# Attention by pairs of heads: 256-column sums over the keys and one bias matmul per span

## The chip, the cores and the metric

The kernel runs on one core of one Trainium2 chip. The metric is the device time of one execution in microseconds (us). A core has TensorE (PE, whose weight loads are shown as PEld), VectorE (DVE), ScalarE (ACT), GpSimd (POOL) and SyncE (SP, which here issues most DMAs). Each engine takes its instructions strictly in the order in which the program lists them.

## The reference, cut to what matters

One decoder block on 1024 tokens of width 1024: an RWKV-7 time mix and a sparse attention run in parallel, are merged, and a product-key expert mixer (PEER) follows. The change touches the attention alone:

```python
kv_sel = c_kv[sel]                     # 256 chosen keys of one shared latent, 8 heads of queries
logits = einsum('bqhd,bqkd->bqhk', qb, kv_sel) * 128 ** -0.5 + rel_bias[t5_bucket(tpos - sel)]
p = softmax(where(valid, logits, -inf))
out = einsum('bqhk,bqkd->bqhd', p, kv_sel)
```

The kernel computes it densely: all causal keys, with a mask that removes those not chosen. All 8 heads share the same keys and values (the latent), so only the queries and the bias differ from head to head.

## The kernel before, in words

The sequence is worked in two halves H of 512 tokens, each of four tiles of 128 queries. In each half, the projections of the input come first (`zphase1`, `zphase2`: weights from HBM, split into a high and a low float32r part by ACT and POOL, and three matmuls on 512 columns for each 128 of depth, lines 424 to 426). Then two kinds of work are listed side by side: `rwkv`, the recurrent mix, whose steps depend on each other (8 chains per half, started 4 steps apart by `staggered`), and `attn`, one generator for each tile and head. Sixteen further projections of `zphase2` (the merge gates) are listed between the heads. After that, `merge_b` projects the attention's output (again lines 424 to 426, eight projections of 24 matmuls), and `merge` needs the output of the last RWKV tile (`rwkv_out`, lines 783 to 812). In the second half, gathers of expert rows (POOL issues, DVE products, line 1395) are tied to steps of `rwkv`. The last half of the time is the dense part of the expert mixer (lines 1290 to 1294).

The program lists the work in this order, but a list scheduler with a clock of its own then sets the order on each engine, so a change in one place moves instructions elsewhere. On PE the order that results is fixed: a matmul that waits holds up all behind it.

`attn(i, h, ap, mask)` does one head of tile i. Its first half: logits of 128 queries against (i+1)*128 keys in spans of at most 512 (line 952, queries `q` stationary), the relative bias of the last two tiles of keys added by one matmul per tile (line 955, `back` stationary), mask and row minimum on DVE (line 958), the exponential and the scaling on ACT (lines 961, 963). Its second half, listed two heads later: each 128x128 block of the probabilities `p` is transposed on PE into a PSUM bank `tp` (line 970), four blocks are copied by ACT to `pT` (line 972; all such copies stand under line 233 in the profile, that of the helper), and one matmul per tile of keys adds up the output, with the values `ckv` stationary and 128 columns moving (line 976). The output is copied to `y1` (named y in the profile) and stored (line 980). PSUM has two banks `tp`, shared by logits and transposes, two banks `acc`, shared by projections and this output, and four banks `rw` for `rwkv`.

```python
heads = [attn(i, h, ap, masks[i]) for i in tiles for h in range(8)]
for n in range(34):
    for g in heads[n:n + 1] + heads[max(0, n - 2):max(0, n - 1)]:
        next(g, None)
```

The functions that the change touches, with the line numbers of the profile:

## Time and profile before

| what | us |
|---|---|
| median of 3 runs | 3731.83 |
| lowest and highest run | 3722.95, 3736.19 |
| the profiled execution, its own time | 3729.43 |
| its span (first to last instruction) | 3727.7 |
| mean granted TensorE clock | 0.972 of full speed |

How to read a profile: an engine's busy time is the time in which it has an instruction in work; matmuls overlap, so PE's busy time counts overlapped ones once. A window row gives, for a stretch of the span, the busy time of each engine with the number of its instructions, the granted clock and the share of the DMA engines. A wait row says which instruction waited, for whom, and how long in total. A timeline row gives the start, the time, the engine, the line, the operation with output and inputs, and the number of instructions merged into it. Every float32 matmul of the code stands as two records in the trace, with two weight loads; a float32r matmul (the projections) stands as one.

### The profile page before, as it was taken

How to read it: one execution, taken by the hardware profiler on the slowest of the kernel's cores; microseconds unless marked ns; L12 is line 12 of the kernel's file. 1: busy time of each engine (PE TensorE's matmuls, PEld its weight loads, DVE VectorE, ACT ScalarE, POOL GpSimd, SP SyncE). 2: the span in 40 equal slices, each digit the busy share in tenths (PEclk: the TensorE clock that was granted, in tenths of full speed). 3: DMA queues.
4: the chain of work that ended last, by engine and by line, in shares of the span. 5: the costliest groups of instructions: out<-in, count | busy, mean ns of one | idle time of the engine just before them, and what ended most of it. 6: DMA issues, size and time to landing. Idle time of an engine off the chain costs nothing.

```text
span 3727.7 us, 64789 instructions
## 1 busy us (share of the span) xinstructions
PE 3499.9 (94%) x24045; PEld 3135.1 (84%) x24045; DVE 2587.5 (69%) x5433; ACT 1694.3 (45%) x3230; POOL 1987.4 (53%) x1572
## 2 busy tenths in 40 slices
PE   8999999889999989879999999999999999999997
PEld 7677777666677767669999999999999999999987
DVE  7856653847467764899989985467667776677654
ACT  3649953244344443447676688422222322222223
POOL 5442222354455554336656542467677676777655
PEclk9999999989999999989999999999999999999999
DMA  7453323864667666478888874889989999898873
GB/s 232 151 159 104 107 87 124 291 194 163 215 206 224 213 213 207 135 230 319 318 327 316 316 284 151 300 320 324 339 317 331 332 330 338 320 332 325 306 263 120
DMA packets 436880, 920.95 MB, mean 247 GB/s; under 512 B 36452, under 2 KB 195508, under 8 KB 433876
## 3 DMA queue, kind: packets, MB, share of 16 engines
q1 hardware_dynamic: 311956, 498.38, 39.8%
q0 software_dynamic: 124608, 418.43, 31.5%
q8 instruction: 189, 3.10, 0.3%
q14 instruction: 127, 1.04, 0.1%
HBM read 791.59 MB, written 125.08 MB: 246 GB/s over the span
## 4 chain that ended last, share of the span: by engine, by line
PE 51%; DVE 15%; DMA 12%; ACT 7%; issue 6%; POOL 6%; SPq 0%; POOLq 0%; ACTq 0%; DVEq 0%
PE pair L1294 8%; PE pair L1292 8%; PE pair L1290 8%; PE acc L424 4%; PE acc L425 4%; PE acc L426 4%; DMA g<-in_u_dram,gidx 4%; DMA g<-in_v_dram,gidx 3%; ACT gt L233 3%; POOL g L1391 2%; DMA raw<-in_ut_dram 2%; POOL wlo L1277 2%; DVE g L1395 2%; PE tp L1264 2%; PE acc L976 1%
## 5 line engine op out<-in xcount | busy, mean ns | idle before, releaser
L1277 POOL TENSOR_TENSOR wlo<-raw,whi 128x1024 fp32r<-128x1024 f32 x264 | 648.7, 2459 | 378.2 <-ACT whi L233 354.5
L414 POOL TENSOR_TENSOR wlo<-wraw,whi 128x512 fp32r<-128x512 f32 x280 | 371.1, 1328 | 550.7 <-ACT whi L233 497.2
L233 ACT ACTIVATE whi<-raw 128x1024 fp32r<-128x1024 f32 x264 | 278.9, 1057 | 649.4 <-PE pair L1292 382.9
L1391 POOL DMA_INDIRECT g<-in_u_dram,gidx x361 | 376.6, 1043 | 293.7 <-DVE g L1395 187.6
L1399 DVE SCALAR_TENSOR_TENSOR pg<-g,dots,pg 128x1024 f32<-128x1024 f32 x317 | 407.0, 1284 | 146.0 <-DMA g<-in_v_dram,gidx 143.0
L1290 PE MATMUL pair<-A,whi 128*128 128x320 f32 (+2 forms) x2048 | 480.5, 311 | 25.4 <-DVE A L1322 19.4
L1290 PE MATMUL pair<-h2T,whi 128*128 128x320 f32 x2048 | 475.6, 312 | 15.0 <-ACT whi L233 15.0
L1292 PE MATMUL pair<-A,whi 128*128 128x320 f32 (+2 forms) x2048 | 479.9, 311 | 3.8 <-DVE A L1322 3.6
L1294 PE MATMUL pair<-A,wlo 128*128 128x320 f32 (+2 forms) x2048 | 478.7, 310 | 0.8 <-POOL wlo L1277 0.8
L1292 PE MATMUL pair<-h2T,whi 128*128 128x320 f32 x2048 | 474.7, 311 | 0.0
L1294 PE MATMUL pair<-h2T,wlo 128*128 128x320 f32 x2048 | 473.1, 311 | 1.6 <-POOL wlo L1277 1.6
L1391 POOL DMA_INDIRECT g<-in_v_dram,gidx x320 | 311.7, 974 | 187.4 <-DVE pg L1399 90.7
L424 PE MATMUL acc<-big,whi 128*128 128x512 f32 x864 | 356.6, 414 | 23.1 <-DVE zs L532 6.5
L1290 PEld LDWEIGHTS pair<-A,whi 128*128 128x128 f32 x2048 | 347.4, 189 | 28.0 <-issue 19.9
L1290 PEld LDWEIGHTS pair<-h2T,whi 128*128 128x128 f32 x2048 | 343.9, 188 | 16.9 <-ACT whi L233 15.4
L426 PE MATMUL acc<-big,wlo 128*128 128x512 f32 x864 | 351.8, 408 | 1.7 <-POOL wlo L414 1.7
L425 PE MATMUL acc<-big,whi 128*128 128x512 f32 x864 | 349.9, 405 | 2.4 <-DVE big L450 2.3
L1292 PEld LDWEIGHTS pair<-A,whi 128*128 128x128 f32 x2048 | 347.4, 189 | 5.1 <-DVE A L1322 5.1
L1395 DVE SCALAR_TENSOR_TENSOR g<-g,pg 128x1024 f32<-128x1024 f32 x233 | 281.3, 1216 | 101.3 <-DMA g<-in_u_dram,gidx 100.2
L1294 PEld LDWEIGHTS pair<-A,wlo 128*128 128x128 f32 x2048 | 347.5, 189 | 1.0 <-POOL wlo L1277 1.0
L1294 PEld LDWEIGHTS pair<-h2T,wlo 128*128 128x128 f32 x2048 | 342.9, 188 | 3.4 <-POOL wlo L1277 2.4
L1292 PEld LDWEIGHTS pair<-h2T,whi 128*128 128x128 f32 x2048 | 344.1, 188 | 0.6
(482 smaller groups left out, 6673.1 us busy)
## 6 DMA issues: line engine op xcount, KB each, us to landing
raw<-in_vt_dram SPq DMA_DIRECT2D x136, 512.0 KB, 4.2
raw<-in_ut_dram SPq DMA_DIRECT2D x128, 512.0 KB, 5.5
gtD<-st SPq DMA_DIRECT2D x20, 2048.0 KB, 9.8
gt<-gtD SPq DMA_DIRECT2D x32, 1280.0 KB, 14.5
wraw<-in_wz_dram SPq DMA_DIRECT2D x152, 256.0 KB, 3.2
dotD<-ds SPq DMA_DIRECT2D x69, 320.0 KB, 5.7
al<-dotD SPq DMA_DIRECT2D x69, 320.0 KB, 6.5
mw<-in_wada_dram SPq DMA_DIRECT2D x32, 512.0 KB, 5.4
```

Of the source, the lines that this page charges most:

```text
L233: copy = lambda o, i, **k: A.activation(o, i, AF.Copy, **k)
L414: G.tensor_tensor(lo, raw, hi.bitcast(F32), op=OP.subtract)
L424: mm(pt, lhsT=wh[:, ks], rhs=ah[:, k, :], start=k == 0, stop=False)
L425: mm(pt, lhsT=wh[:, ks], rhs=al[:, k, :], start=False, stop=False)
L426: ins = mm(pt, lhsT=wl[:, ks], rhs=ah[:, k, :], start=False, stop=k == nk - 1)
L1277: G.tensor_tensor(lo, raw, hi.bitcast(F32), op=OP.subtract)
L1290: mm(pts[n], lhsT=wh, rhs=ah[:, h], start=k == 0, stop=False)
L1292: mm(pts[n], lhsT=wh, rhs=al[:, h], start=False, stop=False)
L1294: latest[:] = [mm(pts[n], lhsT=wl, rhs=ah[:, h], start=False, stop=last)]
L1391: G.indirect_dma_start(out=u, out_offset=None, in_=a["u" if n < 2 else "v"], in_offset=bass.IndirectOffsetOnAxis(ap=idx[:, k:k + 1], axis=0))
L1395: V.scalar_tensor_tensor(u, u, 1.0, h2, op0=OP.mult, op1=OP.mult, accum_out=dots[:, k:k + 1])
L1399: V.scalar_tensor_tensor(acc, u, dots[:, k:k + 1], acc, op0=OP.mult, op1=OP.add)
```

## The change

`attn` now takes two heads, 2*h2_ and 2*h2_+1. It does the first half of one head, pauses, does that of the other, pauses, and then does the second half for both. Two tiles of keys of both heads are transposed into one `tp` bank (four blocks, the two heads of a tile of keys side by side) and copied together, and one matmul with 256 moving columns replaces two with 128. The matmuls of the sums now follow each copy, where before they followed all the copies of a head, and the `acc` bank is taken before the first transpose. The bias of both tiles of keys is one matmul on 256 columns where they lie in the same span of 512 (tiles 1, 2, 3, 5, 6, 7); at tile 4 they lie in two spans and stay apart. The output of both heads is one copy and one store; `y1` has one buffer of 256 columns for two of 128. In the list of work, the second half of a pair stands after the first half of the following pair's first head.

```diff
-    def attn(i, h, ap, mask):
+    def attn(i, h2_, ap, mask):
...
+        pts = []
+        for h in (2 * h2_, 2 * h2_ + 1):
...
-            bt = [k for k in (i - 1, i) if k >= 0 and c0 <= k * 128 < c0 + wd]
-            mm(pl[:, :wd], lhsT=q, rhs=ckvT[:, c0:c0 + wd], start=True, stop=not bt)
-            for k in bt:
-                o = 0 if k == i - 1 else 128
-                mm(pl[:, k * 128 - c0:(k + 1) * 128 - c0], lhsT=back, rhs=bias[:, o:o + 128], start=False,
-                   stop=k == bt[-1])
+                b0, b1 = max(c0, (i - 1) * 128), min(c0 + wd, n)
+                mm(pl[:, :wd], lhsT=q, rhs=ckvT[:, c0:c0 + wd], start=True, stop=b0 >= b1)
+                if b0 < b1:
+                    o = b0 - (i - 1) * 128
+                    mm(pl[:, b0 - c0:b1 - c0], lhsT=back, rhs=bias[:, o:o + b1 - b0], start=False, stop=True)
...
+            pts.append(pt)
+            yield
+        py = pacc()
-        for k0 in range(0, i + 1, 4):
-            kn = min(4, i + 1 - k0)
+        for k0 in range(0, i + 1, 2):
+            kn = min(2, i + 1 - k0)
             tp = ptp()
             for k in range(kn):
-                nc.tensor.transpose(tp[:, k * 128:(k + 1) * 128], pt[:, (k0 + k) * 128:(k0 + k + 1) * 128], ident)
+                for e in range(2):
+                    nc.tensor.transpose(tp[:, (2 * k + e) * 128:(2 * k + e + 1) * 128],
+                                        pts[e][:, (k0 + k) * 128:(k0 + k + 1) * 128], ident)
             pT = ap.tile([128, 512], F32, name="pT", bufs=2)
-            copy(pT[:, :kn * 128], tp[:, :kn * 128])
-            pTs.append(pT)
-        py = pacc()
-        for k in range(i + 1):
-            mm(py[:, 0:128], lhsT=ckv[:, k, :], rhs=pTs[k // 4][:, k % 4 * 128:k % 4 * 128 + 128], start=k == 0,
-               stop=k == i)
-        yb = ap.tile([128, 128], F32, name="y1", bufs=2)
+            copy(pT[:, :kn * 256], tp[:, :kn * 256])
+            for k in range(kn):
+                mm(py[:, 0:256], lhsT=ckv[:, k0 + k, :], rhs=pT[:, k * 256:k * 256 + 256], start=k0 + k == 0,
+                   stop=k0 + k == i)
+        yb = ap.tile([128, 2, 128], F32, name="y1", bufs=1)
...
-                heads = [attn(i, h, ap, masks[i]) for i in tiles for h in range(8)]
+                heads = [attn(i, h, ap, masks[i]) for i in tiles for h in range(4)]
                 for n in range(34):
-                    for g in heads[n:n + 1] + heads[max(0, n - 2):max(0, n - 1)]:
-                        next(g, None)
                     if n < 32:
+                        next(heads[n // 2])
                         zphase2(H, act, range(22 + n * (16 - TAIL) // 32, 22 + (n + 1) * (16 - TAIL) // 32))
+                    if n % 2 == 0 and n > 0:
+                        next(heads[n // 2 - 1], None)
```

The order moves in two places of which the prediction speaks. The first is PE's order at tile 7 in the second half. In the rows of the order, `tp` with `ident` and `p` is a transpose, `tp` with `ckvT` a logit matmul, `tp` with `bias` a bias matmul, `acc` with `pT` a sum over the keys, and `rw` belongs to `rwkv`. Before, for one head and the start of a second:

```order
L955 MATMUL tp<-bias,back 128x128 x2
L694 MATMUL rw<-in 64x64 x8
L719 MATMUL rw<-C,bk 128x64 x8
L699 MATMUL rw<-w,in 64x64 x8
L970 MATMUL tp<-ident,p 128x128 x8
L976 MATMUL acc<-pT,ckv 128x128 x4
L952 MATMUL tp<-ckvT,q 128x512
```

In the changed kernel, at the same steps of `rwkv`:

```order
L955 MATMUL tp<-ckvT,q 128x512 x2
L958 MATMUL tp<-bias,back 128x256
L699 MATMUL rw<-w,in 64x64 x8
L975 MATMUL tp<-ident,p 128x128 x8
L980 MATMUL acc<-pT,ckv 128x256 x2
L975 MATMUL tp<-ident,p 128x128
L694 MATMUL rw<-in 64x64 x8
```

The bias matmuls are one, the sums follow after each copy by twos, and the next transposes follow them without logits in between.

The second place is PE's order at the end of the last chain of `rwkv` in the second half: lines 738, 744, 750, 755 and 756 are its last state step, lines 792, 798, 806 and 807 the normalisation and gate of its output, and `acc` with `big` is a projection of `merge_b`. Before:

```order
L738 MATMUL rw<-sv,pr 64x64 x3
L425 MATMUL acc<-big,whi 128x512
...
L744 MATMUL rw<-rh,w 64x64 x4
L424 MATMUL acc<-big,whi 128x512 x2
...
L750 MATMUL rw<-sv,ed 64x64 x4
...
L792 MATMUL rw<-yall,C 128x128 x2
L426 MATMUL acc<-big,wlo 128x512
...
L798 MATMUL rw<-ss,ind_97 8x128 x4
L426 MATMUL acc<-big,wlo 128x512
...
L806 MATMUL rw<-pr,gnx 128x128
```

In the changed kernel, where `acc` with `Q` is the first projection that needs this chain's output:

```order
L738 MATMUL rw<-sv,pr 64x64 x3
L744 MATMUL rw<-rh,w 64x64 x4
L750 MATMUL rw<-sv,ed 64x64 x4
...
L792 MATMUL rw<-yall,C 128x128 x2
L798 MATMUL rw<-ss,ind_97 8x128 x4
L806 MATMUL rw<-pr,gnx 128x128
L807 MATMUL rw<-gl,g_99 128x128
...
L424 MATMUL acc<-Q,whi 128x512 x2
```

The projections that stood between the steps of this chain stand ahead of it. In the first half the order moves in the same way.

## Rows read from the trace of the kernel before

**Rows 1.** The page, part 1: busy time, share of the span, instructions of each engine.

```profile
PE 3499.9 (94%) x24045; PEld 3135.1 (84%) x24045; DVE 2587.5 (69%) x5433; ACT 1694.3 (45%) x3230; POOL 1987.4 (53%) x1572
```

**Rows 2.** Windows: stretch, its length, busy PE, PEld, DVE, ACT, POOL, clock, DMA share.

```profile
300.00:585.00 285.00, 280.83 (x2761) 223.01 (x2761) 161.68 (x470) 209.97 (x526) 76.62 (x82) 0.98 0.35 103
585.00:656.40 71.40, 64.74 (x481) 46.80 (x479) 25.47 (x50) 21.25 (x46) 17.33 (x15) 0.92 0.39 123
656.40:680.00 23.60, 18.60 (x67) 15.04 (x68) 19.59 (x30) 5.25 (x9) 6.00 (x4) 0.79 0.91 311
950.00:1435.00 485.00, 444.64 (x3836) 346.51 (x3834) 311.92 (x701) 218.21 (x473) 246.90 (x211) 0.96 0.68 212
1435.00:1485.00 50.00, 49.20 (x234) 37.18 (x233) 17.05 (x26) 15.99 (x29) 19.14 (x15) 0.97 0.64 211
```

**Rows 3.** Waits of PE from 950 to 1450 us: total, times, longest.

```profile
PE tp L970 <- DVE asm L958: 15.0, 7, 4.0
PE acc L976 <- ACT pT L233: 4.7, 8, 1.1
PE tp L970 <- ACT pT L233: 4.1, 7, 0.7
```

**Rows 4.** Timeline of PE from 343.6 us: projections, logits, bias and transposes in a row.

```profile
343.64 0.40 PE L424 MATMUL acc<-big,whi 128*128 128x512 f32 x1
343.87 0.40 PE L425 MATMUL acc<-big,whi 128*128 128x512 f32 x1
...
344.35 0.59 PE L952 MATMUL tp<-ckvT,q 128*128 128x256 f32 x2
344.78 0.61 PE L955 MATMUL tp<-bias,back 128*128 128x128 f32 x4
345.23 0.38 PE L970 MATMUL tp<-ident,p 128*128 128x128 f32 x2
```

**Rows 5.** Timeline of PE, end of the last RWKV chain in the second half.

```profile
1436.14 0.45 PE L738 MATMUL rw<-sv,pr 128*64 128x64 f32 x6
...
1454.14 1.04 PE L798 MATMUL rw<-ss,ind 128*8 128x128 f32 x8
...
1464.26 0.49 PE L807 MATMUL rw<-gl,g 128*128 128x128 f32 x2
```

**Rows 6.** Timeline of ACT, DVE and POOL: what that chain does between its matmuls.

```profile
1436.62 0.28 ACT L233 ACTIVATE rh<-rw 128x128 f32<-128x128 f32 x1 [2.17 <-PE rw L738]
...
1444.74 0.28 ACT L233 ACTIVATE yall<-rw 128x128 f32<-128x128 f32 x1 [1.98 <-PE rw L756]
...
1450.04 0.58 ACT L793 ACTIVATE ss<-rw 128x512 f32<-128x512 f32 x1
...
1455.53 0.36 ACT L800 ACTIVATE pr<-rw,eps_gn 8x128 f32<-8x128 f32 x1
...
1455.92 0.94 DVE L801 RECIPROCAL pr<-pr 8x128 f32<-8x128 f32 x1 [3.79 <-ACT pr L800]
...
1464.37 0.69 DVE L808 TENSOR_TENSOR yall<-yall,rw 128x512 f32<-128x512 f32 x1 [5.94 <-PE rw L806]
...
1465.13 1.28 POOL L809 TENSOR_TENSOR yall<-yall,ss 128x512 f32<-128x512 f32 x1 [2.81 <-DVE yall L808]
...
1468.72 0.68 DVE L810 TENSOR_TENSOR yall<-yall,rw 128x512 f32<-128x512 f32 x1
...
1469.44 0.63 ACT L233 ACTIVATE Q<-yall 128x512 fp32r<-128x512 f32 x1
...
1470.55 0.68 DVE L450 TENSOR_TENSOR Q<-yall,Q 128x512 fp32r<-128x512 f32 x1
```

**Rows 7.** The page, part 5: the product of a gathered expert row on DVE.

```profile
L1395 DVE SCALAR_TENSOR_TENSOR g<-g,pg 128x1024 f32<-128x1024 f32 x233 | 281.3, 1216 | 101.3 <-DMA g<-in_u_dram,gidx 100.2
```

**Rows 8.** Timeline of PE just after the first half's RWKV: two projection matmuls.

```profile
660.00 0.63 PE L425 MATMUL acc<-Q,whi 128*128 128x512 f32 x1
660.42 0.63 PE L426 MATMUL acc<-Q,wlo 128*128 128x512 f32 x1
```

More of the change, by code (lines that the diff above doesn't have):

```diff
@@ new lines, in attn @@
+        pts = []
+        for h in (2 * h2_, 2 * h2_ + 1):
+            bias = ap.tile([128, 256], F32, name="bias", bufs=2)
+            nc.sync.dma_start(bias, bass.AP(tensor=biasV.tensor, offset=biasV.offset + h * 384, ap=[[1, 128], [1, 256]]))
+            q = ap.tile([128, 128], F32, name="q", bufs=2)
+            nc.sync.dma_start(q, qD[H][h, :, tt * 128:tt * 128 + 128])
+            sm = ap.tile([128, 4], F32, name="asm", bufs=4)
+            pt = ap.tile([128, 512 * (H + 1)], F32, name="p", bufs=3)
+            first = 3.0e38
+            for c0 in range(0, n, 512):
+                wd = min(512, n - c0)
+                pl = ptp()
+                b0, b1 = max(c0, (i - 1) * 128), min(c0 + wd, n)
[3 more added lines that the diff above has]
+                    mm(pl[:, b0 - c0:b1 - c0], lhsT=back, rhs=bias[:, o:o + b1 - b0], start=False, stop=True)
+                j = c0 // 512
+                V.tensor_tensor_reduce(out=pt[:, c0:c0 + wd], in0=pl[:, :wd], in1=mask[:, c0:c0 + wd], op0=OP.add,
+                                       op1=OP.min, scale=1.0, scalar=first, accum_out=sm[:, j:j + 1])
+                first = sm[:, j:j + 1]
+            A.activation(pt[:, :n], pt[:, :n], AF.Exp, scale=-1.0, bias=first, accum_out=sm[:, 2:3])
+            V.reciprocal(sm[:, 3:4], sm[:, 2:3])
+            copy(pt[:, :n], pt[:, :n], scale=sm[:, 3:4])
+            pts.append(pt)
+            yield
@@ L973, in attn @@
-            pTs.append(pT)
-        py = pacc()
-        for k in range(i + 1):
-            mm(py[:, 0:128], lhsT=ckv[:, k, :], rhs=pTs[k // 4][:, k % 4 * 128:k % 4 * 128 + 128], start=k == 0,
-               stop=k == i)
-        yb = ap.tile([128, 128], F32, name="y1", bufs=2)
-        copy(yb, py[:, 0:128])
-        nc.sync.dma_start(ybD[H][h, :, tt * 128:tt * 128 + 128], yb)
+            copy(pT[:, :kn * 256], tp[:, :kn * 256])
+            for k in range(kn):
+                mm(py[:, 0:256], lhsT=ckv[:, k0 + k, :], rhs=pT[:, k * 256:k * 256 + 256], start=k0 + k == 0,
+                   stop=k0 + k == i)
@@ L983, in load_split @@
+        yb = ap.tile([128, 2, 128], F32, name="y1", bufs=1)
+        copy(yb.rearrange("p a b -> p (a b)"), py[:, 0:256])
+        nc.sync.dma_start(ybD[H][2 * h2_:2 * h2_ + 2, :, tt * 128:tt * 128 + 128].rearrange("h p t -> p h t"), yb)
     def load_split(dst, src, n):
```

19 lines of the change are left out of this document (removed).

## The prediction

> **What bounds the kernel now.** I first read the busy times of the whole page [rows 1]: PE is busy for 94% of the span, so the first question is what the change does to PE's own work, and the second what it does to the little time in which PE waits. The window rows [rows 2] then show the two stretches in which attention runs. In the first half (300 to 585 us) PE is busy for 280.83 of 285 us: there nothing is gained by a shorter wait, only by less work. In the second half (950 to 1435 us) it is busy for 444.64 of 485, so 40 us of idle time lie there, and the waits [rows 3] tell how much belongs to attention: 15.0 us in which transposes (line 970) wait for DVE to free a `tp` bank, 4.1 us in which they wait for ACT's copies, and 4.7 us in which sums (line 976) wait for a copy, 23.8 us in all. Last, the timeline gives what a matmul costs [rows 4], and the order of the changed kernel shows what becomes a neighbour of what.
>
> **PE's own work.** Starts tell the cost, since matmuls overlap. One logit matmul on 256 columns stands as two records, from 344.35 to 344.78 us: 0.43, or 0.215 us a record. Two bias matmuls on 128 columns are four records, from 344.78 to 345.23: 0.45, or 0.112 us each [rows 4]. So two 128-column records cost 0.225 us and the 256-column one that replaces them 0.215: 0.010 us saved. Columns, not instructions, are what is paid for. The sums are 36 tiles of keys times 8 heads, 288 matmuls or 576 records, and become 288: 288 times 0.010 = 2.9 us. The bias is joined for 6 tiles and 8 heads, 48 times, 96 pairs of records: 1.0 us. Together 3.9 us of the span, of which I count 3 (between nothing, if the hundredth is rounding, and 4). Logits and transposes stay as they are.
>
> On this point the Trainium skill speaks for more. Its page "TensorE: Matmul & The Clock Gate" (section "Back-to-back issue gap") gives for a stream of weight loads and matmuls about 81 ns at 128 columns and 131 ns at 512, so that a matmul pays a fixed share beside its columns. By a straight line between the two, an estimate, a 256-column matmul would take 98 ns where two of 128 take 162, and 384 pairs would give 25 us instead of 4. The trace differs: 0.215 against 0.225 us.
>
> **Work taken off other engines.** ACT copies 16 fewer `pT` tiles and 32 fewer outputs, and SP issues 32 fewer stores. I cost this at nothing: ACT is busy for 209.97 of 285 us and PE for 280.83 in the first half [rows 2], so what PE does not wait for is hidden beside it. The cover would fail only if PE waited for these copies, and that is in the waits above. One buffer of `y1` makes a pair's output wait for the store before it, one pair earlier, some 17 us in the first half (285 us over 16 pairs) and 30 in the second (485 over 16): nothing. The `acc` bank is held from a pair's first sum to its last, with one bank left for projections; a projection that ends inside must be copied out before the next begins. The order puts at most one projection's worth of 24 matmuls between a pair's first and last sums, so I take nothing here too; one wait of 0.58 us, the time of an ACT pass over 512 columns [rows 6], for each of 32 pairs, 18 us, is the upper end.
>
> **The waits in attention.** A group of transposes that follows logits waits for DVE to read them out of the bank, and the DVE reading may stand behind a product of a gathered row, 1216 ns each [rows 7]. Before, each head's transposes came after another head's logits. Now, as the first place in the order shows, only a pair's first group does; the rest follows the pair's own sums. I take half of the 15.0 us away, 7.5. The new waits, two sums behind their own copy, have the next four transposes, 0.45 us, ahead of them, as the old ones had; I leave these 4.7 and 4.1 us as they are. The bounds are all 23.8 us gone, or as much again if a pair's chained copies stall PE each time.
>
> **The end of each RWKV part.** This is what is late next. The second place in the order shows that, in the changed kernel, attention and projections move ahead of RWKV, and nothing is left to stand between the last steps of the last chain. Before, 80 projection matmuls stand there (counted in the order), at 0.23 us each [rows 4] 18.4 of the 28.6 us from 1436.14 to 1464.75 [rows 5], and PE is busy for 49.20 of 50 us [rows 2]. They are not lost: they run earlier. But what ACT, DVE and POOL do between the chain's matmuls now becomes idle time of PE: 0.28 and 0.28 (copies), 0.58 (square), 0.36 (root), 0.94 (reciprocal), then after the last matmul 0.69, 1.28, 0.68, 0.63 and 0.68 us until the first merge matmul can start. That is 6.4 us [rows 6]; with the hand-overs and the copies of `sv` between lines 744 and 750, for which I allow 1.6, I take 8. The upper end has two gathered products ahead of it on DVE, 2.4 us more [rows 7], and a clock that falls: after the first half's chain, which is already bare before, the granted clock is 0.79 [rows 2], and matmuls start 0.42 us apart [rows 8] instead of 0.23, so one projection of 24 costs 4.6 us more. The upper end is then 15 us.
>
> In the first half the same end has little cover even before: PE is idle for 6.7 of the 71.4 us from 585 to 656.4 [rows 2]. Now 111 projection matmuls (counted in the order), which stood in the steps before it, are gone from there too, and only the tie-breaking of the indexer remains as cover. The last step and the normalisation cost the same 8 us bare, against the 6.7 now, and the step before them about the same two copies and updates, 1 to 2 us: I take 3 more, between nothing and 10.
>
> **The sum.** Less 3 for PE's work, less 7.5 for attention's waits, plus 8 and plus 3 for the two ends: plus 0.5. The profiled execution took 3729.43 us, so the sum gives 3730; it lies 2.4 us below the median of the runs, 3731.83. What is measured is a median, so I forecast 3732: no change. A measurement of this kernel can tell about 0.3%, 11.2 us, from no change, so "same" means 3720.6 to 3743.0 us. The forecast's own range is 3722 to 3742.
>
> **Rivals.** *The ends outweigh the rest (slower).* The mechanism is the bare end of the RWKV chain, in both halves. It costs 15 us in the second half, by its upper end, and 10 in the first; if attention's waits do not shrink, because a pair's four copies in a row stall as often as the logits did, only 3 us are given back. Then 3731.8 + 22 = 3754. It decides from the point at which the two ends together cost some 14 us more than what attention gives back. For it: the order shows no cover at all, and the clock fell in the first half's end. Against it: the chain could only be late if PE had been the one that delayed it, and projections done early are not done later.
>
> *Attention's waits vanish (faster).* With the copies shared and the transposes in larger groups, all but a few of the 23.8 us go, and the chain of the second half, which shares PE with them, ends earlier by as much, which pays for its bare end. Then 3731.8 - 3 - 19 = 3710. For it: the idle 40 us stand just there. Against it: the largest part is DVE's queue, which the change does not shorten.
>
> *Each load is paid for (faster).* If a record of 128 columns hid a fixed cost as large as half of its 0.112 us, 384 of them would give 21.5 us: 3710. This is the rule that I named above, as a mechanism here. The 256-column logits, with one load for 0.215 us, speak against it.
>
> *It moves, and no more.* The order also shifts by a few places after attention, where DVE and POOL serve gathers and expert tables. That could cost or give 10 us or so by itself, with either sign.
>
> **How the numbers follow.** No change, as summed: 0.44. The ends outweigh: 0.30, at about 3754. The waits vanish: 0.18, at about 3710. Loads: 0.02. Later moves decide: 0.06, half to each side. So faster 0.23, same 0.44, slower 0.33. The range takes in the forecast's own case and reaches most of the way to both others: 3711 to 3757.
>
> **What would show it.** In the profile of the changed kernel: sums on 256 columns start 0.215 us a record apart, and PE's busy time is lower by some 3 us, not 20. Transposes wait for DVE for about half of 15 us. Around the last steps of each half's RWKV, PE stands idle between the lines of the last state step and the first merge matmul, for about 8 us in the second half and about 10 in the first. I am wrong if PE's idle time in attention's second stretch falls by more than 15 us, if the bare ends take more than 25 together, or if the difference lies in the dense part.

## The result, and the profile after

| | before | after |
|---|---|---|
| median of 6 runs each, same chip | 3737.62 us | 3786.32 us |
| lowest to highest | 3722.95 to 3741.05 | 3766.11 to 3796.09 |
| span of the profiled execution | 3727.7 | 3788.8 |
| mean granted clock | 0.972 | 0.956 |

The changed kernel is slower: its time is 1.0136 times that of before, 95% interval 1.0115 to 1.0157. The forecast was no change, 3732 us with a range up to 3757; the time lies above the range. The medians differ by 48.7 us, the two profiled executions by 61.1.

The page of the changed kernel, part 1, in the columns of [rows 1]:

```profile
PE 3532.4 (93%) x23661; PEld 3139.7 (83%) x23661; DVE 2584.6 (68%) x5433; ACT 1689.2 (45%) x3181; POOL 1988.6 (52%) x1572
```

384 matmul records fewer, and yet PE is busy for 32.5 us more. More time for fewer instructions goes with the lower granted clock, 0.956 for 0.972. Windows of the changed kernel show where, in the columns of [rows 2]:

```profile
300.00:585.00 285.00, 278.01 (x2510) 215.38 (x2509) 158.44 (x454) 205.81 (x494) 81.38 (x84) 0.99 0.38 110
605.00:662.50 57.50, 48.60 (x390) 35.41 (x388) 21.22 (x46) 16.33 (x38) 6.68 (x6) 0.67 0.27 85
960.90:1510.56 549.66, 501.91 (x3799) 374.22 (x3798) 314.60 (x715) 228.02 (x473) 269.93 (x223) 0.93 0.64 203
1488.00:1510.60 22.60, 15.14 (x80) 10.17 (x78) 9.07 (x18) 7.26 (x14) 6.03 (x5) 0.65 0.48 152
1510.60:1609.40 98.80, 83.30 (x346) 64.72 (x347) 81.13 (x329) 34.69 (x60) 30.61 (x23) 0.89 0.42 132
```

The third row is the second half's attention stage whole, the fourth its end, the fifth the merge behind it. The same three for before (the stage, the merge, the end):

```profile
956.60:1486.00 529.40, 489.58 (x4060) 382.29 (x4059) 322.53 (x720) 232.48 (x500) 262.34 (x222) 0.96 0.68 212
1486.00:1576.30 90.30, 78.47 (x343) 60.30 (x342) 79.17 (x326) 33.88 (x59) 31.53 (x24) 0.96 0.46 145
1435.00:1485.70 50.70, 49.90 (x237) 37.74 (x236) 17.05 (x26) 15.99 (x29) 19.14 (x15) 0.97 0.63 209
```

I cut the span at marks that both kernels have, and compared stage by stage. A stage called "attention" here begins with RWKV (at its first matmul, line 645, in the first half; at the last matmul ahead of it, line 595, in the second) and ends at the first merge projection (`acc` with `Q`). Its length is 529.4 us before and 549.7 after in the second half (+20.3), 417.0 and 426.2 in the first (+9.2). The second half's merge grows by 8.5 (90.3 to 98.8), the layer norm behind it by 3.5; what lies between the first half's stage and the second's is 4.3 us shorter. All that lies behind the layer norm, the expert mixer, is 24.5 us longer in these two executions; the code there is the same, and this part returns below. Of the 20.3 us in the second half's stage, 7.9 are idle time of PE (39.8 us before, 47.7 after). The other 12.3 are busy time, although PE has some 260 records fewer there, at a granted clock of 0.93 instead of 0.96.

The waits of PE from 960 to 1520 us (first of before, then of after, in the columns of [rows 3]):

```profile
PE rw L694 <- DVE in L688: 8.1, 9, 2.5
```

```profile
PE rw L694 <- DVE in L688: 16.9, 6, 4.5
PE acc L980 <- ACT pT L233: 8.5, 10, 3.6
PE tp L975 <- DVE asm L960: 4.5, 3, 3.1
```

Attention's own waits behaved: transposes wait for DVE 4.5 us where [rows 3] had 15.0, sums wait 8.5 for 4.7. With the small rest that is some 15 us for 23.8, a gain of 8.5 where I had taken 7.5. But RWKV's matmuls (line 694) now wait twice as long, and the other way round POOL waits for them. POOL's waits on them from 957 to 1500 us, before and then after:

```profile
POOL in L689 <- PE rw L694: 16.0, 8, 6.3
```

```profile
POOL in L689 <- PE rw L694: 46.0, 14, 6.4
```

POOL waits for PE three times as long. I read this as PE having become late for RWKV, and the times of RWKV's steps agree. The matmuls of line 744 mark them, 16 steps a half; the last one and the first merge projections, before:

```profile
1439.35 0.45 PE L744 MATMUL rw<-rh,w 64*64 64x64 f32 x8
...
1485.96 0.40 PE L424 MATMUL acc<-Q,whi 128*128 128x512 f32 x1
```

and after, with the bare chain between them (what stands in brackets is the idle time ahead of an instruction and who ended it):

```profile
1492.14 0.45 PE L744 MATMUL rw<-rh,w 64*64 64x64 f32 x8 [0.98 <-ACT rh L233]
...
1496.60 1.22 PE L792 MATMUL rw<-yall,C 128*128 128x128 f32 x4 [0.37 <-ACT yall L233]
...
1498.51 1.87 PE L798 MATMUL rw<-ss,ind 128*8 128x128 f32 x8 [0.69 <-ACT ss L793]
...
1501.90 0.76 PE L806 MATMUL rw<-pr,gnx 8*128 8x128 f32 x2 [1.52 <-DVE pr L801]
...
1510.56 1.22 PE L424 MATMUL acc<-Q,whi 128*128 128x512 f32 x2 [2.84 <-ACT Q L233]
1511.58 0.65 PE L425 MATMUL acc<-Q,whi 128*128 128x512 f32 x1
1512.03 0.63 PE L426 MATMUL acc<-Q,wlo 128*128 128x512 f32 x1
1512.46 0.63 PE L424 MATMUL acc<-Q,whi 128*128 128x512 f32 x1
```

Measured from the start of the stage, the last step comes after 482.8 us before and after 531.2 in the changed kernel, 48.4 later. From it to the merge it is 46.6 us before and 18.5 after, 28.1 less. The difference, 20.3, is the stage's loss. By the order, 150 matmuls of `merge_b`'s projections (the expectations below call them gate projections) stood behind that last step's matmul before, and none now: 34.5 us of work at 0.23 us that moved from behind the step to ahead of it. So of the 48.4 us, 34.5 are moved work and some 14 are lost on the way to the step; and of the 34.5 us that the tail lost in work it gave back only 28.1, so 6.4 are lost in the bare end. Windows from the start of the stage to the last step, before and then after, show what the 14 us are:

```profile
956.55:1439.35 482.80, 443.53 (x3845) 347.15 (x3843) 307.91 (x696) 216.74 (x471) 244.42 (x208) 0.96 0.68 212
```

```profile
960.90:1492.14 531.24, 489.60 (x3739) 365.95 (x3737) 308.17 (x702) 221.55 (x461) 267.55 (x222) 0.94 0.65 205
```

PE's idle time grows by 2.4 us only, from 39.3 to 41.6: what attention's waits gave back, others took. Busy time grows by 46.1 us for 34.5 us of moved work, so nearly all of the 14 us are busy time, at a granted clock of 0.94 instead of 0.96. The steps fall behind long before the bare end: of the 16, the first comes 12.3 us later in its stage than before, the ninth 45.3, and the last seven 40.9 to 51.3. At the ninth, 48 of the 150 moved matmuls stand ahead of it, and the heads have run ahead too.

### The profile page after: what moved, and what is told of

Read it like the earlier page. It is cut to its first block, busy times and chain, and to the rows that moved or that the text cites. A ratio compares the mean times of both kernels' runs of the same rounds, so it can differ in the third digit from the quotient of the medians.

```text
span 3788.8 us, 63890 instructions
## 1 busy us (share of the span) xinstructions
PE 3532.4 (93%) x23661; PEld 3139.7 (83%) x23661; DVE 2584.6 (68%) x5433; ACT 1689.2 (45%) x3181; POOL 1988.6 (52%) x1572
## 3 DMA queue, kind: packets, MB, share of 16 engines
q1 hardware_dynamic: 311444, 498.37, 39.3%
## 5 line engine op out<-in xcount | busy, mean ns | idle before, releaser
L1294 PEld LDWEIGHTS pair<-A,whi 128*128 128x128 f32 x2048 | 350.5, 191 | 39.8 <-issue 32.1
L1294 PEld LDWEIGHTS pair<-h2T,whi 128*128 128x128 f32 x2048 | 343.9, 189 | 17.1 <-ACT whi L233 14.5
L1298 PEld LDWEIGHTS pair<-h2T,wlo 128*128 128x128 f32 x2048 | 343.6, 189 | 0.7
```

The source lines that it names most:

```text
L1294: mm(pts[n], lhsT=wh, rhs=ah[:, h], start=k == 0, stop=False)
L1298: latest[:] = [mm(pts[n], lhsT=wl, rhs=ah[:, h], start=False, stop=last)]
```

## The experiments

The theories with which I began: **A**, the order (the pairs finish earlier in the scheduler's order, projections move ahead, and the RWKV chain ends bare, with idle time and a low clock); **B**, the 256-column matmuls cost something in themselves; **C**, the loss lies in the dense part. All kernels run beside the kernel before on the same chip; its median over the five groups of runs was 3733.4 to 3738.2 us. The last table of this section holds for every kernel the second half's attention stage, cut as above.

**Pairs in one half only.** `attn_one` is the old `attn`; the first kernel has pairs in the second half, the other in the first.

```diff
-                heads = [attn(i, h, ap, masks[i]) for i in tiles for h in range(4)]
+                if H == 1:
+                    heads = [attn(i, h, ap, masks[i]) for i in tiles for h in range(4)]
...
+                else:
+                    heads = [attn_one(i, h, ap, masks[i]) for i in tiles for h in range(8)]
```

> Pairs of heads in the second half alone; the first half's attention as before. Theory A (order: projections run ahead of the second half's RWKV chain, whose end is then bare and at a lower clock): the second half's stages were 21 + 8 + 4 us longer in the changed kernel, so +33 us on the kernel before, 25 to 45, with the first merge matmul of the second half about 20 us later and the first half's stages unchanged. Rival B (the 256-column sums themselves run at a lower clock): the same sign, as this half has 26 of 36 tiles of keys, +30. Rival C (most of the difference is made in the dense part, by another place of its transfers): the stages before the dense part differ by under 10 us, the dense part by 15 to 25.

3793.3 us, ratio 1.0153 (1.0104 to 1.0203): all of the loss, more than A expected.

> Pairs of heads in the first half alone. Theory A: the first half's RWKV end is bare at a lower clock, first merge matmul 8 us later, half of it regained: +4 us, 0 to 10. Rival B (256-column sums lower the clock): 10 of 36 tiles of keys, +10 to 15, spread over the attention stretch. Rival C (dense part): +15 to 25 in the dense part, nothing before it.

3754.3 us, 1.0046 (1.0030 to 1.0062), 16 us above before and above A's range too. The second half is where the change loses most; its attention stage takes 555.2 us in the first kernel and 526.8 in the other, which has the old one there.

**Sums on 128 columns, in pairs.** The changed kernel with each pair's sum as two matmuls.

```diff
-                mm(py[:, 0:256], lhsT=ckv[:, k0 + k, :], rhs=pT[:, k * 256:k * 256 + 256], start=k0 + k == 0,
-                   stop=k0 + k == i)
+                for e in range(2):
+                    mm(py[:, e * 128:e * 128 + 128], lhsT=ckv[:, k0 + k, :],
+                       rhs=pT[:, (2 * k + e) * 128:(2 * k + e + 1) * 128],
+                       start=k0 + k == 0 and e == 0, stop=k0 + k == i and e == 1)
```

> The changed kernel with each sum over a pair taken as two matmuls on 128 columns again (same pairs, same transposes, bias still joined). Theory A (order and bare ends): the order still leaves both RWKV ends bare, so +30 to +50 us, as the changed kernel. Rival B (width lowers the clock): back to within 10 us of the kernel before, with the granted clock of 950 to 1500 us at 0.96 and not 0.93. Rival C: +15 to 25, all in the dense part.

3752.7 us, 1.0044 (1.0024 to 1.0064). Theory A missed; B missed by less, since 14.5 us are above its 10, and its other sign failed: the granted clock from 950 to 1500 us is 0.93, not 0.96. This kernel's order also left 65 of `merge_b`'s matmuls behind the last step, where I had taken it to be as bare as the changed kernel's. By its time it tells the two apart badly.

**Four projections handed over later** (`TAIL = 4` for 0 in the changed kernel: they come behind the heads instead of among them).

> The changed kernel with four of the sixteen projections beside attention listed behind it (TAIL = 4). Theory A: more of RWKV is done before projections run out, in both halves, though the very end stays bare: half of the loss regained, +10 to +30 us. Rival B: no change to the widths, so +45 as the changed kernel. Rival C: +15 to 25 in the dense part.

3767.0 us, 1.0070 (1.0037 to 1.0104): 19 us better than the changed kernel, with 90 matmuls left behind the last step. For A, within its range.

**Holding projections back for the bare end.** The scheduler has a way to say that an instruction may not be issued ahead of another on its engine. `steps_pe` records the last matmul of line 744 of each step.

```diff
-            proj(pt, w, (yb[:, 0], yb[:, 1]), 8)
+            step = [[0, 0, 0, 0, 0, 0, 0, 0], [0, 0, 0, 0, -1, -1, -1, -1]][H][d]
+            with tc.issue_after(steps_pe[H][step].ins) if step else nullcontext():
+                proj(pt, w, (yb[:, 0], yb[:, 1]), 8)
```

This is the smaller hold-back; the larger has `[-3, -2, -1, -1, -1, -1, -1, -1]` for the second half.

> The changed kernel with its last 96 gate projections of the second half (d of 4 to 7) held back until the products of the last RWKV step have been issued; nothing else differs. Theory A (the pairs end attention earlier in the order, the planner moves projections ahead, and the end of the RWKV chain is left bare): the 22.6 us stretch before the merge loses its 7.5 us of idle time and its low clock (0.65), the merge behind it gets back most of its 8.5 us and the layer norm its 3.5, so 3762 to 3772 us; the 11 us lost earlier in that attention stay. Rival B (the pairs are slower in themselves, the end is a bystander): within 5 us of the changed kernel's 3786. Rival D (held-back projections delay the chain itself, since they stand ahead of its matmuls on TensorE): idle time at the end goes but the stretch is as long, 3780 to 3795.

3774.5 us, 1.0102 (1.0051 to 1.0152). Its windows at the end and in the merge:

```profile
1486.00:1508.50 22.50, 20.46 (x96) 15.46 (x94) 7.67 (x11) 9.45 (x16) 9.82 (x8) 1.00 0.63 201
1508.50:1602.60 94.10, 81.04 (x346) 62.53 (x347) 79.11 (x330) 35.06 (x60) 32.07 (x23) 0.91 0.47 146
```

The idle time of the end went from 7.5 to 2.0 us and the clock from 0.65 to 1.00; the merge got back 4.7 us and the layer norm 2.9. The 12 us of the median are less than A's 14 to 24, and the stage itself is no shorter (551.0 us). The interval overlaps that of the changed kernel (1.0115 to 1.0157), so the gain is not clear of the noise.

> As the one before it, but nearly all of the second half's 192 gate projections are held back to the last three RWKV steps, which gives the tail about as many as it had before the change (124 instead of 0 after the products of the last step but for 20); the middle of attention then has none of them. Theory A with the RWKV chain as the bound: the last chain also starts earlier, since nothing stands ahead of it between the steps, and the second half's attention stage comes within 10 us of before: 3750 to 3765 us. Rival E (the pairs leave attention short of cover wherever one takes it from): the idle time only moves from the end into the stretch before it, about 25 us of projections are missing there, and the time is no better than the smaller hold-back, 3765 to 3785.

3798.8 us, 1.0178 (1.0134 to 1.0222): no gain at all, and above the ranges of both. The windows of the stretch ahead, and of the end:

```profile
1400.00:1450.00 50.00, 32.19 (x303) 24.91 (x301) 33.73 (x70) 11.39 (x26) 23.35 (x19) 0.60 0.66 215
1502.00:1524.20 22.20, 22.20 (x98) 17.27 (x97) 7.26 (x11) 6.75 (x14) 9.14 (x8) 1.00 0.75 243
```

The end is full, and the stretch ahead of it stands idle for 17.8 of 50 us at a clock of 0.60. Rival E had the mechanism, at too small a price: the heads and the sixteen projections of `zphase2` run ahead from the start of the stage, and what is taken to the end is missing in the middle. I take a bare end for one place where the loss shows, not for its source.

**Work of no use in the bare end.** After `merge_b`'s last projection, its 24 matmuls are issued three times more, behind the last step; nobody reads the result.

```diff
+            if H in (1,) and d == 7:
+                for _ in range(3):
+                    pt = pacc()
+                    with tc.issue_after(steps_pe[H][-1].ins):
+                        proj(pt, w, (yb[:, 0], yb[:, 1]), 8)
```

> The changed kernel with 72 projections more, whose result nobody reads, put among the last RWKV chain of the second half: work of no use (72 by 0.227 us is 16.3 us), which fills the bare stretch without changing what comes before it. It tells the clock from the order. Theory C (half of the loss is the clock that falls in the bare stretch and stays down in the merge and the layer norm): the stretch itself gains nothing or loses up to 6 us, but its granted clock rises from 0.65 to over 0.85, the merge gets back 6 to 9 us and the layer norm 2 to 4: 3775 to 3782 us. Rival F (the clock behind the stretch doesn't depend on it): the merge stays as slow and the time grows by 0 to 9 us, 3786 to 3796.

3789.6 us, 1.0134 (1.0092 to 1.0176), as the changed kernel.

```profile
1490.00:1520.40 30.40, 26.83 (x147) 20.08 (x145) 7.88 (x18) 7.91 (x15) 5.05 (x4) 0.99 0.36 113
1520.40:1619.10 98.70, 85.92 (x346) 66.34 (x347) 81.96 (x330) 34.26 (x59) 31.32 (x23) 0.87 0.42 132
```

The clock of the end is 0.99, and the merge behind it is as slow as ever, 98.7 us at 0.87. So the theory named C there fell and rival F held: the merge does not owe its low clock to the bare end.

**One part of the change alone.** First the joined bias in the kernel before:

> The kernel before with the joined bias matmul alone, heads one by one as before. Theory A: the order of attention against RWKV is that of before but for 44 bias matmuls fewer, the end keeps its cover, and the time is that of before within what a re-ordered program scatters: 3730 to 3748 us. Rival B (256 columns in one matmul cost clock or wait wherever they stand): 3745 to 3755.

3751.6 us, 1.0045 (1.0023 to 1.0068): above A's range and in B's. Its order had moved too, though, and leaves 100 of `merge_b`'s matmuls behind the last step instead of 150. Then the pairs with the bias in two matmuls:

> The changed kernel with the bias of the two tiles of keys as two matmuls again: the pairs alone. Its order leaves as little for the end as the changed kernel's (at the last RWKV step 26 fewer gate projections are done than in the changed kernel, none is left 20 products later). Theory A (the order): 3770 to 3790 us, most of the changed kernel's loss. Rival B2 (the joined bias, which alone gave 3752, carries a third to a half of the loss): about 3765.

3781.4 us, 1.0132 (1.0106 to 1.0158), in A's range. The pairs alone carry nearly all of the loss.

**The order alone.** These kernels have every instruction of the kernel before and none of the change's. The first hands the two parts of the heads over in the other order, the second hands the projections over ahead of the heads, the third has `TAIL = 4`.

```diff
-                    for g in heads[n:n + 1] + heads[max(0, n - 2):max(0, n - 1)]:
+                    for g in heads[max(0, n - 2):max(0, n - 1)] + heads[n:n + 1]:
                         next(g, None)
```

> The kernel before, every instruction of it, with one line of the attention loop written in the other order: in each step the second part of an earlier head is handed to the planner before the first part of the next head. The planner's order then has 110 gate projections more done by the start of the last RWKV steps, and none left at the end where before had 80; attention itself is as it was, one head at a time, and its bias too. Theory A (what costs is the order that leaves the RWKV chain bare, whoever makes it): 10 to 30 us slower than before, 3745 to 3765. Rival B3 (what costs are the new instructions, the 256-column sums and bias): 3730 to 3740, as before.

3790.8 us, 1.0167 (1.0135 to 1.0198): at least as much as the change, from one line that only changes the order of listing. A had the side, with 30 us at most, and B3 is out.

> A second re-ordering without a new instruction: in each step of the attention loop the projections are handed to the planner before the heads. It leaves the end as bare as the one above by the last step (none left) and 14 projections less bare 40 products earlier. Theory A: 8 to 25 us slower than before, 3743 to 3760. Rival B3: 3730 to 3740.

3776.8 us, 1.0113 (1.0081 to 1.0145), again above A's range.

> A third re-ordering without a new instruction, to the other side: four of the second half's tanh projections are handed over behind attention instead of inside it, so that every RWKV step has 24 to 96 projections fewer done and the last step still has 163 ahead of it where before had 80. Theory A as far as it speaks of the bare end alone: within 8 us of before, the end is covered with plenty, 3730 to 3745. Rival G (any order but the one that the kernel before was tuned to loses, whether it bares the end or not): 3745 to 3765.

3752.3 us, 1.0051 (1.0029 to 1.0072): its attention stages stood within 2.5 us of before, as theory A would have it, but the time is in G's range; the 17 us lie elsewhere. The first one's profile shows the pattern of the changed kernel. Windows of the stage, its end and the merge, then its step and POOL's wait:

```profile
958.40:1502.50 544.10, 493.97 (x4055) 382.48 (x4053) 312.79 (x716) 231.70 (x499) 261.64 (x223) 0.94 0.65 205
1480.00:1502.50 22.50, 17.10 (x85) 11.74 (x83) 7.79 (x15) 9.61 (x16) 5.11 (x5) 0.73 0.50 161
1502.50:1601.60 99.10, 83.73 (x346) 64.84 (x347) 83.67 (x330) 34.81 (x60) 30.47 (x23) 0.89 0.43 131
```

```profile
1481.66 0.45 PE L744 MATMUL rw<-rh,w 64*64 64x64 f32 x8
```

```profile
POOL in L689 <- PE rw L694: 36.7, 16, 4.6
```

The stage is 14.7 us longer, the end bare at 0.73, the merge at 0.89 and 8.8 us longer, the last step 40.5 us later in its stage, POOL's wait more than doubled. No pair and no 256-column sum is in this kernel.

**The instructions of after in the pace of before.** The opposite test. From the order of before I took, for the first logits of each head and for each of a half's 24 projections beside RWKV (16 of `zphase2`, 8 of `merge_b`), the RWKV matmul that it followed; in these kernels it may not be issued ahead of that one. The tables `HEADS` and `GROUPS` hold these places, and `rw_pe` records the matmuls of `rwkv`.

```diff
-            proj(pt, split_w(a["wz"][j], 1024), act, 8)
+            w = split_w(a["wz"][j], 1024)
+            with paced(GROUPS, H, j - 22) if j >= 22 else nullcontext():
+                proj(pt, w, act, 8)
...
+    def paced(table, H, n):
+        at = table[H][n] if H in PACED else None
+        return tc.issue_after(rw_pe[H, at[0]][at[1]].ins) if at else nullcontext()
...
-                mm(pl[:, :wd], lhsT=q, rhs=ckvT[:, c0:c0 + wd], start=True, stop=b0 >= b1)
+                with paced(HEADS, H, tt * 8 + h):
+                    mm(pl[:, :wd], lhsT=q, rhs=ckvT[:, c0:c0 + wd], start=True, stop=b0 >= b1)
...
-            proj(pt, w, (yb[:, 0], yb[:, 1]), 8)
+            with paced(GROUPS, H, 16 + d):
+                proj(pt, w, (yb[:, 0], yb[:, 1]), 8)
```

> The changed kernel, every instruction of it, with the planner held to the pace of before in both halves: the first logits of each head and the first matmul of each of the 24 projections of a half that lie beside RWKV may not be issued ahead of the RWKV matmul that they followed before (a table of places, worked out from the order of before). At the last two RWKV steps 4 to 9 gate projections more are done than before, instead of 144 to 157, and 80 are left 20 products later, as before. Theory A (the order is the whole loss): the loss goes, and what the pairs save shows if it is anything (attention's waits, 7.5 us by the prediction, and 3 us of TensorE's work): 3722 to 3742 us. Rival B (the pairs cost in themselves): 3755 to 3785, since the instructions are those of the changed kernel. Rival G2 (holding back costs as the two hold-backs did, the cover is missing elsewhere): 3765 to 3800.

3760.2 us, 1.0069 (1.0050 to 1.0088): some 22 us of the loss are gone, and the time lies in B's range, not in A's. But the second half's stage takes 530.7 us, as before the change, with the matmuls that took 549.7 free. The first half's takes 426.6, no less than free (426.2; 417.0 before).

> As the one before it, with the projections alone held to the old pace and the heads free to run ahead (they are 2 to 4 logits ahead in the last quarter of the second half). Theory A: the projections at the end are what counts, so within 8 us of the kernel with both held, 3725 to 3750. Rival G2: the heads that run ahead leave the RWKV steps between 2300 and 2600 of the order thin, 10 to 20 us slower than with both held.

3753.1 us, 1.0053 (1.0036 to 1.0070), 3 us above A's range; and not 10 to 20 us slower than with both held, as G2 had it, but 7 lower, with intervals that overlap.

> The kernel before with the joined bias matmul alone, held to the pace of before in the same way: the bias alone gave 3752 us free, with 70 projections more done at the last step than before. Theory A: the order was its whole loss too, 3728 to 3742. Rival B2 (the joined bias costs in itself): stays at 3748 to 3756.

3778.2 us, 1.0126 (1.0105 to 1.0146). Here heads and projections are held. A miss for both: holding made it 27 us slower.

> The kernel before with the attention loop's two parts handed over in the other order (no new instruction; 3791 us free), held to the pace of before in the same way: the control for the holding itself. Theory A: 3728 to 3748, the loss of 55 us goes with the order. Rival G2 (holding has a price of its own, whatever is held): 3755 or more.

3744.7 us, 1.0038 (1.0017 to 1.0058): of the 56 us that the swap costs, some 44 are gone. Holding, again of both, has no great price of its own in this kernel. The last two runs hold the projections alone:

> Pairs and joined bias in the second half alone, with that half's projections held to the pace of before; the first half is that of before, instruction for instruction and in its order. Free, this kernel took 3793 us. Theory A: the second half's attention stage, 529.4 us before and 522.0 in the kernel with both halves held, keeps these 7 us of gain, the merge and the layer norm stand as before, and the first half's 8 us of loss is not there: 3722 to 3738 us, about as fast as before or 10 us faster. Rival H (the 20 us by which the kernel with both halves held still lies above before come from behind the second half, not from the first): 3742 to 3756.

3757.1 us, 1.0054 (1.0033 to 1.0075): rival H, a microsecond above its range. The stage takes 528.7 us, so of the 7 us of gain that A had kept, 0.7 are there. When the expert mixer begins this kernel is 3 us later than before (1668.9 us for 1665.8); the rest of its 22 us comes after that.

> The pairs alone (the bias as two matmuls) in both halves, projections held to the pace of before. Theory A: the joined bias has no price of its own, so as the kernel with both parts held, 3745 to 3760 us. Rival B2 (the joined bias costs in itself, as the bias alone, held, with 3778 us suggests): 3725 to 3742.

3734.6 us, 1.0002 (0.9983 to 1.0020), beside 3734.9 for before. The pairs, which cost 46 us in the scheduler's own order, cost nothing in the pace of before. That is also what B2 expected and not A: without the joined bias the time is 18 us lower than with it. Of that, 5 us stand when the expert mixer begins (1658.0 us for 1663.4), the rest comes behind. Windows of the attention stage, first with both parts of the change and the projections held, then with the pairs alone, held:

```profile
962.60:1484.60 522.00, 485.44 (x3803) 365.76 (x3802) 325.75 (x720) 228.37 (x475) 259.80 (x222) 0.97 0.68 214
```

```profile
953.10:1472.50 519.40, 486.18 (x3856) 373.43 (x3855) 324.42 (x738) 229.42 (x477) 261.06 (x221) 0.96 0.69 215
```

POOL's wait for PE in the same two, and in the joined bias alone with heads and projections held, which stayed slow (line 632 is the one through which all RWKV matmuls go in these kernels):

```profile
POOL in L706 <- PE rw L632: 14.4, 11, 3.1
```

```profile
POOL in L706 <- PE rw L632: 19.4, 10, 4.8
```

```profile
POOL in L706 <- PE rw L632: 45.9, 18, 6.6
```

All kernels but the filled one in a table, from one profile each, in us: the second half's stage, when its last RWKV step comes, how many of `merge_b`'s matmuls the order has behind that step, how long it then takes to the merge, and POOL's wait for RWKV's matmuls, in the line shown above, from 957 to 1500 us. "Both held" is heads and projections; the kernels ran on several chips, beside the kernel before on each.

| kernel | median | stage | last step at | left | step to merge | POOL's wait |
|---|---|---|---|---|---|---|
| before | 3733 to 3738 | 529.4 | 482.8 | 150 | 46.6 | 16.0 |
| after | 3786.3 | 549.7 | 531.2 | 0 | 18.5 | 46.0 |
| pairs, second half only | 3793.3 | 555.2 | 534.1 | 0 | 21.1 | 43.5 |
| pairs, first half only | 3754.3 | 526.8 | 489.9 | 124 | 36.9 | 19.8 |
| sums on 128 columns | 3752.7 | 537.3 | 507.8 | 65 | 29.5 | 45.6 |
| after, four later | 3767.0 | 543.2 | 511.0 | 90 | 32.2 | 38.5 |
| small hold-back | 3774.5 | 551.0 | 517.0 | 96 | 34.0 | 48.0 |
| large hold-back | 3798.8 | 558.4 | 514.1 | 144 | 44.2 | 41.2 |
| bias alone | 3751.6 | 542.2 | 508.0 | 100 | 34.2 | 38.3 |
| pairs alone | 3781.4 | 555.1 | 537.4 | 4 | 17.7 | 51.2 |
| before, swapped | 3790.8 | 544.1 | 523.3 | 17 | 20.8 | 36.7 |
| before, projections first | 3776.8 | 543.9 | 518.2 | 34 | 25.7 | 55.8 |
| before, four later | 3752.3 | 531.8 | 469.7 | 184 | 62.1 | 29.4 |
| after, both held | 3760.2 | 530.7 | 486.5 | 150 | 44.2 | 14.8 |
| after, projections held | 3753.1 | 522.0 | 478.3 | 148 | 43.7 | 14.4 |
| bias alone, both held | 3778.2 | 553.7 | 509.4 | 144 | 44.3 | 45.9 |
| swapped, both held | 3744.7 | 526.3 | 482.1 | 150 | 44.2 | 19.4 |
| second half only, projections held | 3757.1 | 528.7 | 484.6 | 144 | 44.1 | 12.6 |
| pairs alone, projections held | 3734.6 | 519.4 | 473.8 | 144 | 45.6 | 19.4 |

The stages fall into two groups: in every kernel with a stage of 532 us or less POOL waits for PE's RWKV matmuls for less than 30 us, in every one of 537 or more for over 36. The two go together; that POOL's wait is what lengthens the stage is not shown. Held to the old pace, the changed kernel's own instructions run the stage in 522.0 or 530.7 us (projections or both held), beside 529.4 before and 549.7 free.

**What stays open.** First, why the joined bias loses: with both held, it is the one paced kernel whose stage stays long, although at its first and last RWKV step as many projections and heads are done as before; the second parts of the heads and all other engines were not held, and no run holds them. Of the changed kernel's 48.7 us, 20 to 27 are still there in its two held forms, and the first half's stage stays 6.6 and 9.6 us longer than before in them; with the pairs alone it is 3.4 shorter. The joined bias matmul is not dearer, as the next section shows. Second, the time behind the layer norm. It is 2061.9 us before and 2 to 26 us longer in the other profiles, 20.2 in the changed kernel with projections held and 8.1 in the pairs held, whatever the change in front. PE's order can be left out for its dense part, from the first matmul on `A` to the last on `h2T`: there it is the same in all twenty profiles, and the part took 1234.7 us before, 1247.7 after, and 1234.1 to 1245.7 in the others. Single runs of before alone lie between 3713.96 and 3751.53 us, so one profile each can't tell scatter from a cost there.

## Why the prediction was wrong

**PE's own work: next to nothing, as forecast, but the saving is not shown.** The sums on 256 columns in the changed kernel, with logits and a joined bias behind them:

```profile
1259.90 0.59 PE L980 MATMUL acc<-pT,ckv 128*128 128x256 f32 x2
1260.33 0.81 PE L955 MATMUL tp<-ckvT,q 128*128 128x384 f32 x2
1260.98 0.59 PE L958 MATMUL tp<-bias,back 128*128 128x256 f32 x2
```

Two records take 0.43 us, 0.215 each, as forecast from [rows 4]. But most of the sums come in runs of four, which start 0.24 us apart in the median, and that is more than the 0.225 of the two records that each replaces. In the stage PE is busy for 485.44 us with the projections held, at a clock of 0.97, against 489.58 at 0.96 before. That is a few microseconds, some of which may be the clock's, and the rival in which each load is paid for, 21.5 us, is out. On the rule of the Trainium skill that spoke for it (page "TensorE: Matmul & The Clock Gate", section "Back-to-back issue gap"): the measured 0.215 and 0.24 us a record speak against carrying its figures over to these matmuls.

**The waits in attention: right in themselves.** About 15 us are left of 23.8, a gain of 8.5 for a forecast of 7.5. That it shortens the stage is not shown: in the four held kernels with pairs in the second half, the stage is 10.0, 7.4 and 0.7 us shorter than before and 1.3 longer.

**The end of each RWKV part: right for the second half's bare end, and yet the step that failed.** I had 8 us for the second half, 15 at most; the bare end loses 6.4 (7.5 us of idle time, with a clock of 0.65 beside it). The first half's attention grew by 9.2 us for a forecast of 3 with an upper end of 10, but not where I had put it: from its last step to the merge it takes 19.0 us before and 19.7 after, and the rest stands ahead of that step. The granted clock of its last 57.5 us is 0.67, where [rows 2] has 0.92 from 585.00 to 656.40; the forecast of 3 had no term for that. What failed is the sentence against the slow rival, "the chain could only be late if PE had been the one that delayed it, and projections done early are not done later". Its second half is true: 28.1 of 34.5 us came back. Its first half is true as well, and PE was the one. In a fixed order each projection and head that moves ahead of an RWKV matmul makes that matmul later, and POOL, which waits for it, with it (46.0 us for 16.0). The steps ahead of the last one lost 14 us, where I had nothing: I looked for the price of the bare end alone. That the order makes this loss is shown by the runs on the order alone and by the held pairs. How it makes it is not: of the 14 us, 2.4 are idle time of PE, and the rest is the same work in more busy time at the lower clock.

**What lies behind it** I had at nothing too. The merge is 8.5 us longer. It is 3.8 to 9.7 us longer in every kernel whose order leaves 100 matmuls or fewer behind the last step, also without a pair, and between 1.9 shorter and 2.1 longer in all that leave 124 or more. The layer norm adds 3.5, and the mixer behind it the 24.5 of which the section above leaves the cause open. The clock of the end is not the cause of the longer merge, since filling the end did not help; the cause itself was not settled.

**The rivals.** The slow one, at 3754 us and 0.30, had the right side and less than half of the price, 22 us of 48.7, since it also took its sum from the ends. "It moves, and no more", at 0.06, named the larger thing: that the order shifts, with either sign. But I placed it behind attention and valued it at 10 us. A re-ordering with no new instruction costs 42 and 56 us in two of three cases. The three signs of failure that I had named: idle time in attention did not fall; the bare ends did not take over 25 us together; 13 us of the difference between the two profiles do lie in the dense part, and of those no cause is shown.

## What to carry to other kernels

Where a scheduler sets the order and a dependent chain runs beside filler work, cost a change by what it moves ahead of the chain's instructions: look at the chain's step times and at who waits for its matmuls, not only at the stretch that is left bare. Before blaming or praising a new instruction, run two controls: the old instructions in a shifted order, and the new ones held to the old order. Here 8.5 us less of waiting in attention were worth nothing, since the same edit moved 34.5 us of work from one side of the chain's last step to the other; and even in the old order the pairs gained nothing that the runs can tell (1.0002).

## What was not expected of the hardware

The clock of a stretch did not follow from that of the stretch ahead of it. With the bare end filled its granted clock was 0.99, and the merge behind it still ran at 0.87; with the middle starved (0.60 over 50 us), the end after it ran at 1.00. Nor did a stretch's idle time alone give its clock: up to the last step PE idles for 39.3 us before and 41.6 after, and the clock is 0.96 and 0.94. At the lower of the two levels, 1.2 GHz, projections start 0.43 us apart (1512.03 and 1512.46 in the changed kernel's merge), at the higher, 2.4 GHz, 0.23 ([rows 4]). And 7.5 us of idle time, spread over a chain's hand-overs, stood in a stretch of 22.6 us at a granted clock of 0.65: nearer the lower level (0.5) than the higher.
